# Per-head sums and their spreading in four strips of TensorE: an RWKV and pooling decoder layer

## The chip, the cores and the metric

The kernel runs on one core of a Trainium2 chip. Its time is the device time of one execution in microseconds (us). In this text PE is TensorE (the matrix engine), DVE is VectorE, ACT is ScalarE, POOL is GpSimd and SP is SyncE, which issues the loads here. PE reads its operands from SBUF and writes to PSUM, whose unit here is a bank of 128 rows by 512 numbers of fp32.

## What is computed

One decoder layer on 256 tokens and 2048 channels, all in float32: a mixer, a feed-forward block with squared ReLU, and a gate by a per-layer embedding, each added to the residual stream, with a final norm. Half of the mixer's channels go through causal averages over four windows, the other half, 16 heads of 64 channels, through RWKV-7:

```python
kk = hs(k * k_k)
kk = kk / jnp.maximum(jnp.linalg.norm(kk, axis=-1, keepdims=True), 1e-12)
k = k * (1.0 + (a - 1.0) * k_a)
...
y = wkv7_scan(r_h, hs(decay), k_h, v_h, -kk, kk * a_h)
mu = jnp.mean(y, axis=-1, keepdims=True)
var = jnp.mean(jnp.square(y - mu), axis=-1, keepdims=True)
y = (y - mu) * lax.rsqrt(var + GN_EPS) * gn_g + gn_b
y = y + jnp.sum(r_h * k_h * r_k, axis=-1, keepdims=True) * v_h
```

`hs` splits the channels into heads. The change touches two places of this: the norm of `kk` over the 64 channels of each head (one number for each head and token), which is spread back over the 64 channels, and the last line, a sum over the channels of a head that is spread over them and multiplied by the values. That second term is called the bonus below.

## The kernel before

**Stages.** The mixer fills the first 360 us of the execution, then come the feed-forward block and the gate. Everything after the mixer is the same in both kernels.

**Layout.** The 16 heads are worked on as two groups of 8 (index `gi`, 0 and 1). A group has 512 channels, held as 4 tiles of 128 channels (the partitions) by 256 tokens: `tile[:, p, t]`, p from 0 to 3, two heads in each p. Tiles from the pool `rp` have tags (`tA` to `tF`, `sq` and so on), and a later tile of the same tag waits until the earlier one is no longer read.

**Products of the weights.** A product in full fp32 precision is made of three faster ones: weights and activations are split into a high and a low half (`wh` + `wl`), and `prod_cols` (L176 to L178) and `prod_toks` (L185 to L187) multiply high by high, high by low and low by high. `split_w` makes the halves of a weight panel of 128 x 1024: ACT copies the high half in two pieces (L163), DVE subtracts it to get the low half (L164). The halves lie in rings of three buffers. The products z (`zk`, `zr`, `zv` of each group, and `zp`, the pooled half) take 8 panels each. The small sums and transposes of the mixer are plain fp32 matmuls, for which the trace shows two records each.

**Order.** PE's order is the order of the Python program (`manual_schedule`). The z products are generators in a queue. `fill(us)` takes as many of their products as fill the given time by its own table, 0.36 us for three products of 256 columns and 0.68 for three of 512, and `finish(gen)` runs the queue up to the end of one product. So the order of the main program (L913 to L965) sets at which point of the stream of z products each small step of the mixer stands. The other engines are ordered by a scheduler with priorities: the panels' splits have 20000 and a few steps of `rwkv_k` 30000. `beside` holds a triangular inverse that runs on DVE (L652, L656), one step for each 1.65 us of fill.

**Banks.** The z products use four PSUM banks of the pool `psm`, all small steps of the mixer four of the pool `psr` (`rw_bank`), in turn.

**The norm, `rwkv_k`.** The squares `sq` (ACT) are summed over the heads in 8 fp32 matmuls with the squares as weights and `jhead` (128 x 2, which tells the two heads of a tile) as data (L524); the result has tokens on the partitions and 16 columns. After the maximum and reciprocal on DVE (L527, L529) and the root on ACT, two transposes (L533) bring it to 8 rows (heads) by 256 tokens. These are split into a high half (ACT, L168) and a low half (DVE, `rnp`, L169), and 8 matmuls with `hsel` (L543, L544) spread them over the channels, two tiles p into each of two banks. `kkn` is the product with `zk` and `k_k` (DVE, L548). `rnp` has the tag `tE`, as has `k2`, made from L552 on ACT and L555 on DVE, so `k2` waits for the spreading. `BK` (L567, L568) and `AR` (L569) are built from `kkn` and `k2`.

**The bonus, in `rwkv_values`.** `rk` is the product of r, k and `r_k`. `block_sum` multiplies it by `jsum` (128 x 128, ones where row and column are of one head): sum and spreading in one step, two fp32 matmuls of 512 columns (L463), and DVE multiplies each by the values (L706, `bon`, in the buffer of `rk`). In the same function eight matmuls `vt` (L699) make the centred and transposed values.

**Other steps that are named below.** `rwkv_lora` (L480 to L505): decay and rate of a group, small products `lw` and `la` (L491) into a bank each, then ACT, scans and exponentials. `rwkv_scores` and `rwkv_sources` (`bkt`, L628). `rwkv_merge`: 32 products `gm` (L680) and 32 products `qm` (L687). `rwkv_core`: the recurrence over blocks of 64 tokens (`sm` L767, `rym` L780). `pool_mix`: the pooled half (`pm` on PE, `mp` on ACT L901 and DVE L902).

## Time and profile before

| | us |
|---|---|
| median of three runs | 1205.45 |
| lowest and highest | 1203.94 and 1206.46 |
| the profiled execution, its own time | 1204.86 |
| its span, first to last instruction | 1203.1 |
| PE busy | 1183.2 |
| DVE busy | 872.9 |
| ACT busy | 674.7 |

The mean clock granted to PE is 0.997 of the full one. The trace belongs to the one profiled execution, and what is worked out from it is set against that execution's own time. Rows of the timeline give start, duration, engine, line and operation, then the tiles as out<-in with their sizes and types. A row that ends in square brackets had its engine idle before it, for so long and until the named operation released it. Matmuls overlap in the array, so a row's duration can be longer than the distance to the next row. Rows of the windows give the window, its length, and the busy time of each engine in it with the number of instructions.

### The profile page before, as it was taken

The numbers are of one execution on the slowest core, as the hardware profiler recorded it, in microseconds if no ns is written. First come the engines' busy times: TensorE is split into PE (matmuls) and PEld (weight loads), VectorE is DVE, ScalarE is ACT, GpSimd is POOL, SyncE is SP. The second block draws the span as 40 slices with busy tenths as digits, with TensorE's granted clock in tenths as the row PEclk, the third lists the DMA queues.
The fourth block names the chain that finished last, engine by engine and source line by source line (L and its number), as shares of the span: only waits on it lengthen the run. The fifth ranks groups of instructions, "written<-read, shape, count | busy, mean of one in ns | idle before, by whom it ended". The sixth has DMA issues, their size and how long they took to land.

```text
span 1203.1 us, 18401 instructions
## 1 busy us (share of the span) xinstructions
PE 1183.2 (98%) x7070; PEld 1015.0 (84%) x7070; DVE 872.9 (73%) x1186; ACT 674.7 (56%) x1203; POOL 15.5 (1%) x65
## 2 busy tenths in 40 slices
PE   7999999999999999999999999999999999999997
PEld 5999988987888888888888888888888887887886
DVE  6887987964566666666878887666667788788753
ACT  5957556565545545555545554555555555468743
POOL 3100000000000000000000000000000000000000
PEclk9999999999999999999999999999999999999999
DMA  7363543354365565565656666665565666666841
GB/s 275 124 195 113 175 141 107 107 187 142 120 211 175 175 192 184 185 191 180 192 200 205 206 194 217 185 191 181 187 192 168 194 205 204 229 203 200 271 139 70
DMA packets 60616, 216.88 MB, mean 180 GB/s; under 512 B 6768, under 2 KB 7536, under 8 KB 60144
## 3 DMA queue, kind: packets, MB, share of 16 engines
q1 hardware_dynamic: 60240, 215.20, 55.5%
q8 instruction: 55, 0.90, 0.3%
q10 hardware_dynamic: 288, 0.51, 0.1%
q14 instruction: 33, 0.27, 0.1%
HBM read 213.59 MB, written 2.10 MB: 179 GB/s over the span
## 4 chain that ended last, share of the span: by engine, by line
PE 89%; DVE 6%; DMA 2%; ACT 2%; issue 1%; ACTq 0%; DVEq 0%
PE u_w L1016 20%; PE d_p L1085 15%; PE u_w L1020 10%; PE d_w L1085 4%; PE d_d L1085 4%; DMA raw_d<-in_w_ffn_down_dram 2%; PE gt_b L187 2%; PE gt_b L186 2%; PE gt_b L185 2%; PE wag_b L346 1%; PE zp_b L185 1%; PE zv_b L176 1%; PE zp_b L187 1%; PE zp_b L186 1%; PE o_b L186 1%; PE o_b L185 1%
## 5 line engine op out<-in xcount | busy, mean ns | idle before, releaser
L1016 PE MATMUL u_w<-h,wh_u 128*128 128x512 f32 x1024 | 362.1, 399 | 0.0
L1020 PE MATMUL u_w<-h,wl_u 128*128 128x256 f32 x1024 | 287.7, 281 | 0.0
L164 DVE TENSOR_TENSOR wl_u<-raw_u,wh_u 128x1024 fp32r<-128x1024 f32 x128 | 156.7, 1224 | 122.2 <-ACT wh_u L163 122.2
L163 ACT ACTIVATE wh_u<-raw_u 128x512 fp32r<-128x512 f32 x256 | 147.6, 624 | 173.4 <-issue 137.0
L1016 PEld LDWEIGHTS u_w<-h,wh_u 128*128 128x128 f32 x1024 | 192.4, 188 | 47.9
L1020 PEld LDWEIGHTS u_w<-h,wl_u 128*128 128x128 f32 x1024 | 193.4, 189 | 0.0
L1085 PE MATMUL d_p<-wh_d,yd 128*128 128x512 f32 x480 | 154.5, 389 | 0.8 <-ACT wh_d L163 0.8
L163 ACT ACTIVATE wh_d<-raw_d 128x512 fp32r<-128x512 f32 x160 | 89.1, 620 | 36.8 <-issue 18.5
L1085 PEld LDWEIGHTS d_p<-wh_d,yd 128*128 128x128 f32 x480 | 90.1, 188 | 20.0 <-ACT wh_d L163 1.2
L164 DVE TENSOR_TENSOR wl_d<-raw_d,wh_d 128x1024 fp32r<-128x1024 f32 x80 | 95.4, 1220 | 14.3 <-ACT wh_d L163 13.9
L1085 PE MATMUL d_p<-wl_d,yd 128*128 128x512 f32 x240 | 93.6, 390 | 0.0
L1085 PE MATMUL d_d<-wh_d,yd 128*128 128x512 f32 x160 | 55.8, 389 | 0.0
L1085 PEld LDWEIGHTS d_p<-wl_d,yd 128*128 128x128 f32 x240 | 45.1, 188 | 9.7 <-DVE wl_d L164 0.6
L1138 ACT ACTIVATE th_d<-t_d 128x1024 fp32r<-128x1024 f32 x24 | 25.4, 1058 | 47.6 <-DVE t_d L1135 30.2
L1085 PE MATMUL d_w<-th_d,ys 128*128 128x512 f32 x144 | 48.2, 389 | 0.0
L1142 ACT ACTIVATE th_d<-t_d 128x1024 fp32r<-128x1024 f32 x24 | 25.4, 1059 | 35.4 <-DVE t_d L1140 31.2
L1143 DVE TENSOR_TENSOR tl_d<-t_d,th_d 128x1024 fp32r<-128x1024 f32 x24 | 29.4, 1225 | 19.9 <-ACT th_d L1142 19.6
L1132 ACT ACTIVATE w7h_d<-raw_d 128x1024 fp32r<-128x1024 f32 x24 | 25.4, 1059 | 23.4 <-DMA raw_d<-in_w_ffn_down_dram 13.8
L187 PE MATMUL gt_b<-wh_gt,h 128*128 128x512 f32 x96 | 37.8, 393 | 0.0
L176 PE MATMUL zv_b<-hTh,wh_zv 128*128 128x256 f32 x128 | 37.7, 294 | 0.0
L176 PE MATMUL zr_b<-hTh,wh_zr 128*128 128x256 f32 x128 | 37.5, 293 | 0.0
L185 PE MATMUL gt_b<-wh_gt,h 128*128 128x512 f32 x96 | 37.5, 390 | 0.0
(582 smaller groups left out, 2622.8 us busy)
## 6 DMA issues: line engine op xcount, KB each, us to landing
raw_u<-in_w_ffn_up_dram SPq DMA_DIRECT2D x128, 512.0 KB, 3.5
raw_d<-in_w_ffn_down_dram SPq DMA_DIRECT2D x128, 512.0 KB, 3.9
raw_gt<-in_w_ple_gate_dram SPq DMA_DIRECT2D x24, 512.0 KB, 4.2
raw_zk<-in_w_in_dram SPq DMA_DIRECT2D x16, 512.0 KB, 3.4
raw_zr<-in_w_in_dram SPq DMA_DIRECT2D x16, 512.0 KB, 3.5
raw_zv<-in_w_in_dram SPq DMA_DIRECT2D x16, 512.0 KB, 3.4
raw_zp<-in_w_in_dram SPq DMA_DIRECT2D x16, 512.0 KB, 3.4
raw_o<-in_w_out_dram SPq DMA_DIRECT2D x16, 512.0 KB, 4.1
```

Source lines behind the costliest of these rows:

```text
L163: nc.scalar.activation(wh[:, a * 512 : (a + 1) * 512], raw[:, a * 512 : (a + 1) * 512], AF.Copy)
L164: nc.vector.tensor_tensor(wl, raw, wh.bitcast(F32), op=ALU.subtract)
L176: nc.tensor.matmul(o, w_h, ah, start=first and ct % 2 == 0, stop=False, skip_group_check=True)
L185: nc.tensor.matmul(o, a_h, wh[:, 0:n], start=first, stop=False)
L186: nc.tensor.matmul(o, a_h, wl[:, 0:n], start=False, stop=False)
L187: nc.tensor.matmul(o, a_l, wh[:, 0:n], start=False, stop=last)
L1016: nc.tensor.matmul(bank[:, ct, :].rearrange("p (s t) -> p s t", s=2), wh[:, c], hl, start=k == 0, stop=False, skip_group_check=True,)
L1020: nc.tensor.matmul(bank[:, ct, 0:T], wl[:, c], hl[:, 0, :], start=False, stop=k == 15, skip_group_check=True)
L1085: nc.tensor.matmul(o, l, r, start=first, stop=last, skip_group_check=True)
L1132: nc.scalar.activation(ha, ra, AF.Copy)
L1138: nc.scalar.activation(th[0], t[0], AF.Copy)
L1143: nc.vector.tensor_tensor(tl[1], t[1], th[1].bitcast(F32), op=ALU.subtract)
```

## The change

Sums over a head and their spreading are two steps now, each of four matmuls that use 32 rows or 32 columns of PE's array.

- `head_sums` (new): weights are a slice of 32 columns of `jsel` (128 x 46, zeros with the two head columns in the middle), data a tile of 128 channels by n tokens; the tile p goes to the strip of 32 columns p, that is to the rows 32p to 32p+31 of one bank. For the norm the tokens are cut into 8 pieces of 32, and each piece lands in its own two rows of the strip by the slice of `jsel`: 32 matmuls of 32 columns, and a result of 128 x 32, so that the maximum, the root and the reciprocal work on 32 columns. For the bonus there is one piece: 4 matmuls of 256 columns.
- `head_spread` (new): the rows 32p to 32p+31 of `hsel` (now 128 x 128) as weights and the same rows of the sums as data, four fp32 matmuls of 256 columns, each on its own strip of rows, into four banks.
- In the norm a product with `qmask` on DVE (tile `rnq`, 128 x 256) puts the 8 pieces in their columns. The transposes, the split and the tile `rnp` are gone, and with them the wait of `k2`. The fills become 6.4 and 4.6 (they were 5.4, 3.2 and 1.8).
- The bonus leaves `rwkv_values`. `bonus_sums` stands behind `rwkv_sources`, with a copy to SBUF on ACT; `bonus` spreads the sums and multiplies each bank with the values on DVE, four products of 128 x 256. For group 0 it stands behind a new fill(5.0), ahead of `rwkv_lora(1)`, for group 1 ahead of `rwkv_merge(1)`.
- `rwkv_values(0)` moves from ahead of `rwkv_scores(1)` to behind `rwkv_merge(0)`; the fill behind it is 3.0 (it was 1.5).

```diff
@@ -93,16 +93,15 @@
-    jsum = mc.tile([128, 128], F32, name="jsum")
     cmask = mc.tile([128, 128], F32, name="cmask")
...
     make_block_diagonal(nc, cmask, 64)
-    nc.gpsimd.tensor_copy(jsum, cmask)
     cen = mc.tile([128, 128], F32, name="cen")
-    nc.vector.scalar_tensor_tensor(cen, jsum, -1.0 / 64.0, ident, op0=ALU.mult, op1=ALU.add)
-    jhead = mc.tile([128, 2], F32, name="jhead")
-    nc.gpsimd.tensor_copy(jhead, cmask[:, ::64])
+    nc.vector.scalar_tensor_tensor(cen, cmask, -1.0 / 64.0, ident, op0=ALU.mult, op1=ALU.add)
+    jsel = mc.tile([128, 46], F32, name="jsel")
+    nc.gpsimd.memset(jsel, 0.0)
+    nc.gpsimd.tensor_copy(jsel[:, 14:16], cmask[:, ::64])
@@ -294,12 +293,17 @@
-    hsel_f = rp.tile([8, 512], F32, tag="BKt", name="hsel_f")
-    nc.gpsimd.memset(hsel_f, 1.0)
-    nc.gpsimd.affine_select(hsel_f, hsel_f, [[1, 512]], ALU.is_ge, 0.0, base=0, channel_multiplier=-64)
-    nc.gpsimd.affine_select(hsel_f, hsel_f, [[-1, 512]], ALU.is_ge, 0.0, base=63, channel_multiplier=64)
-    hsel = mc.tile([8, 512], F32R, name="hsel")
-    nc.gpsimd.tensor_copy(hsel, hsel_f)
+    hsel = mc.tile([128, 128], F32, name="hsel")
+    nc.gpsimd.memset(hsel[0:32], 0.0)
+    for q in range(8):
+        nc.gpsimd.affine_select(hsel[0:32], hsel[0:32], [[-1, 2], [0, 64]], ALU.not_equal, 1.0, base=-2 * q, channel_multiplier=1)
+    qmask = mc.tile([128, 8, 32], F32, name="qmask")
+    nc.gpsimd.memset(qmask[0:32], 1.0)
+    nc.gpsimd.affine_select(qmask[0:32], qmask[0:32], [[-2, 8], [0, 32]], ALU.is_ge, 0.0, base=0, channel_multiplier=1)
+    nc.gpsimd.affine_select(qmask[0:32], qmask[0:32], [[2, 8], [0, 32]], ALU.is_ge, 0.0, base=1, channel_multiplier=-1)
+    for p in range(1, 4):
+        nc.gpsimd.tensor_copy(hsel[p * 32 : (p + 1) * 32], hsel[0:32])
+        nc.gpsimd.tensor_copy(qmask[p * 32 : (p + 1) * 32], qmask[0:32])
@@ -455,13 +459,25 @@
-    def block_sum(src, name, consume):
-
-        s = flat(src)
-        for hf in range(2):
-            b = rw_bank("bsum")
-            nc.tensor.matmul(b, jsum, s[:, hf * 512 : (hf + 1) * 512], start=True, stop=True)
-            consume(hf, b)
+    def head_sums(src, name, pieces):
+
+        b = rw_bank(name)
+        n = T // pieces
+        for q in range(pieces):
+            for p in range(4):
+                nc.tensor.matmul(
+                    b[p * 32 : (p + 1) * 32, 0:n], jsel[:, 14 - 2 * q : 46 - 2 * q], src[:, p, q * n : (q + 1) * n],
+                    start=q == 0, stop=q == pieces - 1, skip_group_check=True,
+                )
+        return b[:, 0:n]
+
+    def head_spread(src, name):
+
+        banks = [rw_bank(f"{name}{p}")[:, 0:T] for p in range(4)]
+        for p in range(4):
+            r = slice(p * 32, (p + 1) * 32)
+            nc.tensor.matmul(banks[p], hsel[r], src[r], start=True, stop=True)
+        return banks
 
@@ -512,41 +528,23 @@
                 nc.scalar.activation(sq[:, p, :], zk[:, p, :], AF.Square, scale=col("k_k", 4 * gi + p))
         nc.scalar.activation(warm, sq[:, 3, 0:1], AF.Sqrt)
 
-        fill(5.4)
-        nb = rw_bank("kkn")
...
-        rn = rp.tile([128, 16], F32, tag="rn", name=f"rn{gi}")
+        fill(6.4)
+        nb = head_sums(sq, "kkn", 8)
+        rn = rp.tile([128, 32], F32, tag="rn", name=f"rn{gi}")
+        rnq = rp.tile([128, T], F32, tag="sq", name=f"rnq{gi}")
         with tc.high_priority(30000):
-            nc.vector.tensor_scalar_max(rn, nb[:, 0:16], 1e-24)
+            nc.vector.tensor_scalar_max(rn, nb, 1e-24)
             nc.scalar.activation(rn, rn, AF.Sqrt)
             nc.vector.reciprocal(rn, rn)
-        fill(3.2)
-        nb = rw_bank("rnT")
-        for tt in range(2):
-            nc.tensor.transpose(nb[0:8, tt * 128 : (tt + 1) * 128], rn[:, tt * 8 : tt * 8 + 8], ident)
-        rnh, rnl = (t_[0:8, 0:T] for t_ in pair_tile("tE", f"rnp{gi}"))
-        with tc.high_priority(30000):
-            split_sb(rnh, rnl, nb[0:8, 0:T])
-        fill(1.8)
-        for half in range(2):
-            b = rw_bank("rnb")
...
+            nc.vector.tensor_tensor(
+                rnq.rearrange("r (q t) -> r q t", q=8), rn.unsqueeze(1).to_broadcast([128, 8, 32]), qmask, op=ALU.mult
+            )
+        fill(4.6)
+        rnb = head_spread(rnq, "rnb")
+        for p in range(4):
+            with tc.high_priority(30000):
+                nc.vector.scalar_tensor_tensor(
+                    kkn[:, p, :], zk[:, p, :], col("k_k", 4 * gi + p), rnb[p], op0=ALU.mult, op1=ALU.mult
                 )
@@ -689,6 +687,18 @@
+    def bonus_sums(gi, st):
+        nb = head_sums(st["rk"], "bsum", 1)
+        st["bs"] = rp.tile([128, T], F32, tag="sq", name=f"bs{gi}")
+        with tc.high_priority(30000):
+            nc.scalar.activation(st["bs"], nb, AF.Copy)
+
+    def bonus(st, zv):
+        bon = st["rk"]
+        for p, b in enumerate(head_spread(st["bs"], "bon")):
+            with tc.high_priority(30000):
+                nc.vector.tensor_tensor(bon[:, p, :], b, zv[:, p, :], op=ALU.mult)
+
     def rwkv_values(gi, st, zv):
 
         uvs = [rp.tile([128, 2, 8, 64], F32, tag=f"q{i}", name=f"UV{gi}_{i}") for i in range(2)]
@@ -699,14 +709,6 @@
                 nc.scalar.activation(flat3(UV[2 * tt + i])[64:128], b[i * 64 : (i + 1) * 64, :], AF.Copy)
-        bon = st["rk"]
-        bf, vf = flat(bon), flat(zv)
-        block_sum(
-            st["rk"], f"rk{gi}",
-            lambda hf, b: nc.vector.tensor_tensor(
-                bf[:, hf * 512 : (hf + 1) * 512], b, vf[:, hf * 512 : (hf + 1) * 512], op=ALU.mult
-            ),
-        )
         st["UV"] = UV
 
     def rwkv_core(gi, st):
@@ -929,7 +931,10 @@
     rwkv_scores(0, st0)
     beside += [inverse(0, st0), 1.65, 0.0]
     rwkv_sources(0, st0)
+    bonus_sums(0, st0)
     finish(p_zv0)
+    fill(5.0)
+    bonus(st0, zv0[0])
     st1 = rwkv_lora(1)
     finish(p_zk1)
     rwkv_k(1, st1, zk1[0])
@@ -937,16 +942,17 @@
     rwkv_r(1, st1, zr1[0])
     run(beside.pop(0) if beside else ())
     beside.clear()
-    rwkv_values(0, st0, zv0[0])
     fill(7.0)
     rwkv_scores(1, st1)
     rwkv_merge(0, st0)
     beside += [inverse(1, st1), 0.95, 0.0]
-    fill(1.5)
+    rwkv_values(0, st0, zv0[0])
+    fill(3.0)
     core0 = rwkv_core(0, st0)
     mg0 = a8(0, "mg0", F32R)
     rwkv_out(0, *rwkv_norm1(0, *core0), mg0)
     rwkv_sources(1, st1)
+    bonus_sums(1, st1)
     finish(p_zp0)
     ds0 = pool_chunk(0, pool[0])
     pws0 = pool_weights(0)
@@ -955,6 +961,7 @@
     mixes = [pool_mix(0, ds0, pws0), None]
     run(beside.pop(0) if beside else ())
     beside.clear()
+    bonus(st1, zv1[0])
     rwkv_merge(1, st1)
     rwkv_values(1, st1, zv1[0])
 
```

PE, around the lora of group 1, before: `zv` ends, the lora comes at once, and the products of `zk` for group 1 begin behind it.

```order
L177 MATMUL zv_b_972<-hTl_160,wh_zv_7_1261 128x256
L178 MATMUL zv_b_972<-hTh_158,wl_zv_7_1262 128x256
L491 MATMUL lw<-zf,wa_1322 128x256 x2
L491 MATMUL la<-zf,wa_1322 128x256 x2
L176 MATMUL zk_b_1336<-hTh_157,wh_zk_0_1340 128x256
L177 MATMUL zk_b_1336<-hTl_159,wh_zk_0_1340 128x256
L178 MATMUL zk_b_1336<-hTh_157,wl_zk_0_1341 128x256
```

PE, the same place after: `bsum` stands within the last panel of `zv`, and nearly two panels of `zk` are done when the four spreading matmuls (`bon`) and the lora come.

```order
L176 MATMUL zk_b_1376<-hTl_158,wh_zk_1_1415 128x256
L177 MATMUL zk_b_1376<-hTh_156,wl_zk_1_1416 128x256
L479 MATMUL bon_1440<-bs_1345,hsel 128x256
L479 MATMUL bon_1441<-bs_1345,hsel 128x256
L479 MATMUL bon_1442<-bs_1345,hsel 128x256
L479 MATMUL bon_1443<-bs_1345,hsel 128x256
L507 MATMUL lw<-zf,wa_1452 128x256 x2
L507 MATMUL la<-zf,wa_1452 128x256 x2
L175 MATMUL zk_b_1377<-hTh_156,wh_zk_1_1415 128x256
```

The four `bon` banks are the four of the pool, so that `lw` and `la` take the banks of the first two next.

DVE at that place, before (`tmp` and `X` are steps of the inverse, `wl_zk_3` is the low half of the fourth panel of `zk`, the rows L498 are the lora's scans):

```order
L498 SCALAR_TENSOR_TENSOR tB_t<-rmask,tA_t 128x256
L652 TENSOR_TENSOR tmp_1232<-X_1231,AT_1230 64x175
L498 SCALAR_TENSOR_TENSOR tB_t<-rmask,tA_t 128x256
L656 TENSOR_TENSOR X_1231<-X_1231,tmp_1232 64x7x25
L652 TENSOR_TENSOR tmp_1232<-X_1231,AT_1230 64x192
L498 SCALAR_TENSOR_TENSOR tB_t<-rmask,tA_t 128x256
L656 TENSOR_TENSOR X_1231<-X_1231,tmp_1232 64x8x24
L498 SCALAR_TENSOR_TENSOR tB_t<-rmask,tA_t 128x256
L652 TENSOR_TENSOR tmp_1232<-X_1231,AT_1230 64x207
L656 TENSOR_TENSOR X_1231<-X_1231,tmp_1232 64x9x23
L652 TENSOR_TENSOR tmp_1232<-X_1231,AT_1230 64x220
L164 TENSOR_TENSOR wl_zk_3_1465<-raw_zk_3_1462,wh_zk_3_1464 128x1024
```

DVE there after:

```order
L650 TENSOR_TENSOR tmp_1279<-X_1278,AT_1277 64x175
L654 TENSOR_TENSOR X_1278<-X_1278,tmp_1279 64x7x25
L163 TENSOR_TENSOR wl_zk_3_1531<-raw_zk_3_1528,wh_zk_3_1530 128x1024
L650 TENSOR_TENSOR tmp_1279<-X_1278,AT_1277 64x192
L700 TENSOR_TENSOR ybuf<-bon_1440,zv_t 128x256
L700 TENSOR_TENSOR ybuf<-bon_1441,zv_t 128x256
L654 TENSOR_TENSOR X_1278<-X_1278,tmp_1279 64x8x24
L700 TENSOR_TENSOR ybuf<-bon_1442,zv_t 128x256
L700 TENSOR_TENSOR ybuf<-bon_1443,zv_t 128x256
L650 TENSOR_TENSOR tmp_1279<-X_1278,AT_1277 64x207
```

The bonus products (L700) stand behind `wl_zk_3` and one step of the inverse, and the lora's scans come later.

DVE in the second `rwkv_k`, before, from the transposes that end the inverse (`T1G`) on:

```order
L661 STREAM_TRANSPOSE T1G_1993<-X_1231 32x16x32 x2
L169 TENSOR_TENSOR rnp_1783<-rnT,rnp_1783 8x256
L164 TENSOR_TENSOR wl_zr_5_1876<-raw_zr_5_1873,wh_zr_5_1875 128x1024
L665 STREAM_TRANSPOSE tmp_1232<-X_1231 64x16x32
L548 SCALAR_TENSOR_TENSOR tB_t<-zk_t,par_sb,rnb 128x256 x4
L164 TENSOR_TENSOR wl_zr_6_1909<-raw_zr_6_1906,wh_zr_6_1908 128x1024
L566 TENSOR_TENSOR tF_t<-tB_t,tD_t 128x1024
L555 TENSOR_TENSOR tE_t<-tE_t,zk_t 128x1024
L164 TENSOR_TENSOR wl_zr_7_1944<-raw_zr_7_1941,wh_zr_7_1943 128x1024
L567 TENSOR_TENSOR BK_1828<-tF_t,tC_t 128x16x64
L164 TENSOR_TENSOR wl_zp_0_2027<-raw_zp_0_2024,wh_zp_0_2026 128x1024
L568 TENSOR_TENSOR BK_1828<-tE_t,tC_t 128x16x64
```

DVE there after:

```order
L650 TENSOR_TENSOR tmp_1279<-X_1278,AT_1277 64x135
L553 TENSOR_TENSOR tE_t<-tE_t,zk_t 128x1024
L163 TENSOR_TENSOR wl_zr_2_1791<-raw_zr_2_1788,wh_zr_2_1790 128x1024
L163 TENSOR_TENSOR wl_zr_3_1865<-raw_zr_3_1862,wh_zr_3_1864 128x1024
L566 TENSOR_TENSOR BK_1912<-tE_t,tC_t 128x16x64
L654 TENSOR_TENSOR X_1278<-X_1278,tmp_1279 64x27x5
L536 TENSOR_SCALAR rn_1836<-kkn 128x32
L163 TENSOR_TENSOR wl_zr_4_1925<-raw_zr_4_1922,wh_zr_4_1924 128x1024
L538 RECIPROCAL rn_1836<-rn_1836 128x32
L650 TENSOR_TENSOR tmp_1279<-X_1278,AT_1277 64x112
L539 TENSOR_TENSOR rnq_1837<-rn_1836,qmask 128x256
L654 TENSOR_TENSOR X_1278<-X_1278,tmp_1279 64x28x4
```

The product for `k2` (L553) and the slot of `BK` made from it (L566) stood behind the spreading (L555, L568), and stand now ahead of the norm's steps, with the panels `wl_zr_2` and `wl_zr_4` behind the one and the other.

At the merge of group 1 the four `bon` of group 1 stand between the last product of the pool mix and `gm`, which takes one of their banks next.

More of the change, by code (lines that the diff above doesn't have):

```diff
@@ L513, in rwkv_k @@
         nc.scalar.activation(warm, sq[:, 3, 0:1], AF.Sqrt)
-        fill(5.4)
-        nb = rw_bank("kkn")
-        for hf in range(2):
-            h = flat(sq)[:, hf * 512 : (hf + 1) * 512]
-            for j in range(2):
-                for tt in range(2):
-                    o = tt * 8 + (2 * hf + j) * 2
-                    ts_ = slice(j * T + tt * 128, j * T + (tt + 1) * 128)
-                    first = hf == 0 and j == 0 and tt == 0
-                    nc.tensor.matmul(nb[:, o : o + 2], h[:, ts_], jhead, start=first, stop=True, skip_group_check=True)
@@ L531, in rwkv_k @@
-        nb = rw_bank("rnT")
-        for tt in range(2):
-            nc.tensor.transpose(nb[0:8, tt * 128 : (tt + 1) * 128], rn[:, tt * 8 : tt * 8 + 8], ident)
-        rnh, rnl = (t_[0:8, 0:T] for t_ in pair_tile("tE", f"rnp{gi}"))
-        with tc.high_priority(30000):
-            split_sb(rnh, rnl, nb[0:8, 0:T])
-        fill(1.8)
-        for half in range(2):
-            b = rw_bank("rnb")
-            for j in range(2):
-                p = half * 2 + j
-                o = b[:, j * T : (j + 1) * T]
-                nc.tensor.matmul(o, hsel[:, p * 128 : (p + 1) * 128], rnh, start=j == 0, stop=False, skip_group_check=True)
-                nc.tensor.matmul(o, hsel[:, p * 128 : (p + 1) * 128], rnl, start=False, stop=True, skip_group_check=True)
-            for j in range(2):
-                p = half * 2 + j
-                with tc.high_priority(30000):
-                    nc.vector.scalar_tensor_tensor(
-                        kkn[:, p, :], zk[:, p, :], col("k_k", 4 * gi + p), b[:, j * T : (j + 1) * T], op0=ALU.mult, op1=ALU.mult
+            nc.vector.tensor_tensor(
+                rnq.rearrange("r (q t) -> r q t", q=8), rn.unsqueeze(1).to_broadcast([128, 8, 32]), qmask, op=ALU.mult
+            )
```

## Prediction

> **What bounds the kernel now.** I read the shares by engine first, then the chain of waits, then the waits of TensorE (PE), then the stage of the change (100 to 180 us) in windows.
>
> ```profile
> PE 1183.2 (98%) x7070; PEld 1015.0 (84%) x7070; DVE 872.9 (73%) x1186; ACT 674.7 (56%) x1203; POOL 15.5 (1%) x65
> PE 89%; DVE 6%; DMA 2%; ACT 2%; issue 1%; ACTq 0%; DVEq 0%
> PE rnb L544 <- DVE rnp L169: 0.7, 1, 0.7
> 110.00:120.00 10.00, 10.00 (x83) 9.28 (x80) 9.79 (x24) 9.30 (x18) 0.00 (x0) 1.00 0.30 97
> 120.00:130.00 10.00, 9.93 (x83) 9.72 (x82) 9.59 (x21) 6.06 (x11) 0.00 (x0) 1.00 0.53 166
> 130.00:140.00 10.00, 10.00 (x86) 10.00 (x85) 9.69 (x21) 4.39 (x10) 0.00 (x0) 1.00 0.57 188
> 150.00:160.00 10.00, 10.00 (x71) 9.87 (x71) 9.43 (x12) 5.43 (x10) 1.10 (x2) 0.83 0.44 140
> 152.20:155.40 3.20, 3.20 (x18) 3.20 (x17) 3.20 (x5) 1.66 (x5) 0.00 (x0) 0.50 0.34 129
> 170.00:180.00 10.00, 10.00 (x64) 7.93 (x64) 6.79 (x9) 4.93 (x11) 0.00 (x0) 1.00 0.35 118
> ```
>
> The first two rows say that the end is set by PE's own work: 98% busy, 89% of the chain. So an instruction taken off PE shortens the kernel, unless something else is late behind it. The window rows (length, then busy time of PE, weight load, DVE, ACT, POOL, then the granted clock) say where that may happen: from 110 to 160 us VectorE (DVE) is busy 9.4 to 9.8 of every 10 us. There PE and DVE bound the kernel together, and only after 170 has DVE room again (6.79). Two more things stand in this stage: one wait of PE of 0.7 us in rnb, and a stretch at half clock, 152.2 to 155.4 us, that loses 3.2 x 0.5 = 1.6 us.
>
> How closely PE follows DVE there, two rows tell: the low half of a weight panel is done at 122.31 + 1.21 = 123.52, and PE's first product with it starts at 123.58.
>
> ```profile
> 122.31 1.21 DVE L164 TENSOR_TENSOR wl_zk<-raw_zk,wh_zk 128x1024 fp32r<-128x1024 f32 x1
> 123.58 0.38 PE L178 MATMUL zk_b<-hTh,wl_zk 128*128 128x256 f32 x1
> ```
>
> **What the change takes off PE.** Each block is read from its first row to the first regular product behind it.
>
> ```profile
> 59.02 1.84 PE L524 MATMUL kkn<-jhead,tF_t 128*128 128x2 f32 x16
> 60.72 0.36 PE L176 MATMUL zr_b<-hTh,wh_zr 128*128 128x256 f32 x1
> 64.04 0.38 PE L533 MATMUL rnT<-ident,rn 128*8 128x128 f32 x2
> 66.28 0.28 PE L178 MATMUL zr_b<-hTh,wl_zr 128*128 128x256 f32 x1
> 66.49 0.38 PE L543 MATMUL rnb<-rnp,hsel 8*128 8x256 f32 x1
> 67.62 0.39 PE L176 MATMUL zr_b<-hTh,wh_zr 128*128 128x256 f32 x1
> 148.56 0.38 PE L543 MATMUL rnb<-rnp,hsel 8*128 8x256 f32 x1
> 149.61 0.38 PE L544 MATMUL rnb<-rnp,hsel 8*128 8x256 f32 x1 [0.67 <-DVE rnp L169]
> 150.63 0.39 PE L176 MATMUL zr_b<-hTh,wh_zr 128*128 128x256 f32 x1
> 165.87 1.88 PE L463 MATMUL bsum<-ybuf,jsum 128*128 128x512 f32 x4
> 167.82 0.40 PE L186 MATMUL zp_b<-wl_zp,hTh 128*128 128x512 f32 x1
> ```
>
> There are two groups of heads, so each of these runs twice. Norm sums (kkn): 60.72 - 59.02 = 1.7 us, and 0.1 for the change of shape ahead of it (66.49 - 66.28 = 0.21 us into rnb, where 83 matmuls in a window of 10 us make 0.12 the pace): 1.8, both groups 3.6. Transposes (rnT): between 0.1 and 0.38, I take 0.2, both 0.4; they go altogether. Spreading (rnb): 67.62 - 66.49 = 1.1 and 0.1 ahead, 1.2 in group 0; 150.63 - 148.56 = 2.1 and 0.1 ahead, 2.2 in group 1, which holds the wait. Bonus sums (bsum): 167.82 - 165.87 = 1.95, less about 0.25 for the zp product that lies inside, 1.7; both 3.4. Sum of what goes: 3.6 + 0.4 + 3.4 + 3.4 = 10.8 us.
>
> **What it adds on PE.** The new products work on a 32-wide strip of the array each, and no row of before has four strips. The nearest rows have two, or one:
>
> ```profile
> 45.07 0.48 PE L491 MATMUL lw<-zf,wa 64*128 64x256 f32 x1
> 45.08 0.48 PE L491 MATMUL la<-zf,wa 64*128 64x256 f32 x1
> 45.39 0.38 PE L491 MATMUL lw<-zf,wa 64*128 64x256 f32 x1
> 45.60 0.38 PE L491 MATMUL lw<-zf,wa 64*128 64x256 f32 x1
> 202.58 0.69 PE L767 MATMUL sm<-UV,BKt 128*64 128x64 f32 x16
> 203.11 1.10 PE L780 MATMUL rym<-UV,SC 128*64 128x64 f32 x16
> 204.13 0.39 PE L176 MATMUL zv_b<-hTh,wh_zv 128*128 128x256 f32 x1
> 262.36 2.21 PE L680 MATMUL gm<-T1G,SC 32*32 32x32 f32 x64
> 264.50 0.50 PE L185 MATMUL zp_b<-wh_zp,hTh 128*128 128x512 f32 x1
> ```
>
> lw and la use different halves of the rows of the array and start 0.01 us apart: they run together, and a pair of records takes 45.39 - 45.07 = 0.32 us the first time and 45.60 - 45.39 = 0.21 then. sm alternates between strips, 16 records in 203.11 - 202.58 = 0.53 us; rym has the same shape on one strip, 16 in 1.02. So strips do overlap. An fp32 product leaves two records (64 in the row of gm for 32 products).
>
> A quad of four products of 256 columns (bsum, rnb and bon) is 8 records. If four strips run together it is two such beats, 0.3 and 0.2, and 0.2 for the change of shape in and out: 0.7 us. If they run one after the other it is 0.3 + 7 x 0.2 + 0.2 = 1.9. The pairs say together: I take 0.7. Six quads: 4.2 us. The new kkn is 32 products of 32 columns, 64 records. At the pace of gm, 264.50 - 262.36 = 2.14 us for 64 records on one strip, or 0.033 us each, they take 2.1 and with the shape 2.3; with four strips side by side a quarter, 0.5 and 0.3 for the shape, 0.8. I take 1.0 each, near the lower end because lw and la start 0.01 us apart; both 2.0. The Trainium skill speaks against that: TensorE: Matmul & The Clock Gate, section Back-to-back issue gap, gives a floor of about 25 ns from one product to the next however short it is. By it the 64 records would take an estimated 1.6 us, and the sum below would come out 1.8 us worse; the 10 ns between lw and la are under that floor, the 33 ns of sm are above it.
>
> PE's work: 4.2 + 2.0 - 10.8 = -4.6 us, the 0.7 of the wait among it.
>
> **The half clock.** Of all that PE waits for in this stage only the rnb wait precedes it, by 2.6 us. In the new form there is no transpose between the norms and their spreading: the mask product follows the reciprocal on DVE at once, and 4.6 us of z products cover what 3.2 + 1.8 covered with the transposes between. So I let the wait go, and the half clock with it: -1.6 us. Bounds: 0 and -1.6. The Trainium skill (the same page, section HAM oscillation — how this bites in real kernels) has the clock fall after idle of more than about 3.4 us. By that rule this stretch isn't due to a wait of 0.67 us and would stay, and the sum would be 1.6 us worse; the trace can't decide it: the stretch stands behind that wait, but the wait of h3t, quoted below, has none behind it.
>
> **What it gives back.** The change makes PE wait for DVE at three new places, since the spread takes all four banks of the rw pool at once, and the next user needs DVE to have emptied one.
>
> ```profile
> 112.03 1.21 DVE L164 TENSOR_TENSOR wl_zk<-raw_zk,wh_zk 128x1024 fp32r<-128x1024 f32 x1
> 113.16 0.47 DVE L310 SCALAR_TENSOR_TENSOR zv_t<-zv_b,par_sb,zv_t 128x255 f32<-128x255 f32 x1
> 155.54 1.21 DVE L555 TENSOR_TENSOR tE_t<-tE_t,zk_t 128x1024 f32<-128x1024 f32 x1
> 160.74 1.22 DVE L568 TENSOR_TENSOR BK<-tE_t,tC_t 128x1024 f32<-128x1024 f32 x1
> 170.65 1.27 DVE L706 TENSOR_TENSOR ybuf<-bsum,zv_t 128x512 f32<-128x512 f32 x2
> 262.57 0.89 DVE L902 SCALAR_TENSOR_TENSOR mp<-pm,par_sb,mp 128x256 fp32r<-128x256 f32 x2 [0.54 <-ACT mp L901]
> ```
>
> (a) Bonus of group 0, then lora(1). On DVE the four bonus products stand behind a weight panel (1.21 us) and one small operation of the triangular inverse (0.3); each is a DVE operation of 128x256 out of PSUM, of 0.4 us in a row (0.47 alone, as the zv_t row). lw needs the first bank. If DVE takes the panel when the quad begins, lw waits 1.2 + 0.3 + 0.4 - 0.7 = 1.2 us, and la 0.4 longer behind the second: 1.4 with both. Bounds: 0 if DVE is done with the panel by then, 2.0 if it begins it late. Queued behind on PE is everything; on ACT the lora's exponentials, which have until rwkv_k(1).
>
> (b) DVE work pulled ahead of the second rwkv_k. The bonus moves from 170 us, where DVE has room, to 115, where it has none: 4 x 0.4 = 1.6 us (before, two operations of twice the width, 1.27). The product for k2 (1.21) and the second slot of BK (1.22) no longer wait behind rnp (its tile is gone) and now stand ahead of weight panels of zr, as the order of DVE shows. That is 4.0 us in front of panels, and the one quoted above has a margin of 0.06 us. Against it stand the wait (a), in which DVE catches up, and the rnp pair and two small norms that go. What PE saves before 160 must also be made by DVE: it can't start a panel earlier than DVE has it. Bounds: 0, and 2.4 (the pulled-ahead pair in full). I take 1.0.
>
> (c) Bonus of group 1, then merge(1). gm now needs a bank that DVE empties behind two operations of the pool mix, which end at 262.57 + 0.89 = 263.46; the bonus product makes it 263.9. Without the wait gm would begin the quad's 0.7 later than its 262.36 of before, at 263.1. So about 0.7 us more. Bounds: 0 and 0.9.
>
> What moves without a price: vt of group 0 goes behind merge(0), with fill(3.0) to cover its copies; ACT is 5 to 6 of 10 us busy there. The copies of the bonus sums (a 128x256 on ACT, under 0.5 us each) have 5 us of z products over them; without that cover the first bon would wait 0.5. POOL builds its masks at the start; on SP the lora's weight load moves behind one more panel's load, and its first use behind 5 us more of products.
>
> **The sum.** -4.6 - 1.6 + 1.4 + 1.0 + 0.7 = -3.1 us; from the profiled execution's 1204.86 us (span 1203.1) to 1201.8. That execution is 0.6 below the median of 1205.45, so from the median it would be 1202.4. I take 1202.2.
>
> **Rivals.** (1) The new waits don't come: DVE is ahead where I see it behind, since PE starts a little later at each place. For it: ACT delivers wh early now; against: 9.4 to 9.8 of 10. 1204.86 - 6.2 = 1198.7. (2) DVE swallows it: all that PE saves before 160 is waited for at the panels. What stays are the two bsum quads of 1.7 taken behind 160 (3.4), less the bonus quad and sums of group 1 (1.4) and (c) 0.7, less the bonus's own 1.6 us on DVE now in the bound stretch: -3.4 + 1.4 + 0.7 + 1.6 = +0.3, 1205.2. For it: the 0.06 us margin of the panel; against: at 170 us DVE has room again, and what it does there can slip. (3) Short products issue one after the other: kkn 2.3 each instead of 1.0, 1202.2 + 2.6 = 1204.8. (4) Slower: idle costs clock. One wait of 0.67 us stood ahead of a stretch that lost 1.6. The change has waits at four places (lw of (a), two panels of (b), gm of (c)). With none of them followed by half clock it stands at 1202.2; each that is adds 1.6: 1203.8, 1205.4, 1207.0, 1208.6. From the second on nothing is won, at the third it is slower. For it: the stretch at 152; against: the longest wait on another engine, at h3t, where no half clock follows:
>
> ```profile
> 1101.31 0.66 PE L1037 MATMUL h3t<-ident,x 128*128 128x128 f32 x4 [0.82 <-DVE h L1044]
> 1104.00:1108.00 4.00, 4.00 (x23) 3.26 (x22) 2.91 (x7) 3.87 (x11) 0.00 (x0) 1.00 0.43 141
> ```
>
> (5) Four strips don't run together: 6 x 1.2 + 2.6 = 9.8 more, 1212.0; against: sm at half the time of rym. (6) The change doesn't do what it says for the wait: rnq is as late as rnp was, and the wait and the half clock stay: 1202.2 + 0.7 + 1.6 = 1204.5.
>
> **How the numbers follow.** About 0.2% (2.4 us) is what a measurement tells from no change. Forecast 0.42, with its own range from 1200.8 to 1203.6; rival 1 0.22; 2 0.11; 3 0.06; 4 0.12; 5 0.03; 6 0.04. Faster (under 1203.0): 0.36 of the forecast and all of 1, 0.58. Same: 0.06 of the forecast, 0.09 of rival 2, all of 3 and 6, 0.25. Slower: 4, 5 and the rest of 2, 0.17. The range goes from 1198.6 to 1207.2: it takes in 1 to its point and 4 up to its third step, and leaves out 5, the end of 4 and the lower side of 1.
>
> **What would show it.** Right: the spread quads as 8 records within 0.8 us, four starts within 0.05 us; kkn near 1.0; no PE wait at rnb and a clock of 1.00 in all windows from 140 to 170; PE waits of about a microsecond at lw (on DVE's bonus) and 0.7 at gm. Wrong: a quad of 1.9 us; kkn over 2; new rows of half clock behind the lw wait; PE waits on wl_zk or wl_zr that add up to more than 2 us; or no waits at all at lw and gm.

## The result and the profile after

The changed kernel takes 1207.22 us (median of 17 runs, 1205.35 to 1212.11); before took 1203.94 (17 runs, 1200.04 to 1206.48). The ratio is 1.0036, with a 95% interval from 1.0024 to 1.0047: slower, by 3.3 us by the medians and about 4 by the ratio. The profiled execution took 1207.79 us, with a span of 1206.1.

TensorE's own work first. In the timeline of after, the new blocks:

```profile
60.34 0.28 PE L177 MATMUL zr_b<-hTh,wl_zr 128*128 128x256 f32 x1
60.55 0.76 PE L468 MATMUL kkn<-tF_t,jsel 128*32 128x32 f32 x64
61.24 0.39 PE L175 MATMUL zr_b<-hTh,wh_zr 128*128 128x256 f32 x1
66.10 0.71 PE L479 MATMUL rnb<-rnq,hsel 32*128 32x256 f32 x8
66.75 0.39 PE L175 MATMUL zr_b<-hTh,wh_zr 128*128 128x256 f32 x1
114.09 0.71 PE L479 MATMUL bon<-bs,hsel 32*128 32x256 f32 x8
115.86 0.70 PE L507 MATMUL lw<-zf,wa 64*128 64x256 f32 x2 [1.06 <-DVE ybuf L700]
```

The norm's sums, 64 records, take 61.24 - 60.55 = 0.69 us, where the 16 records of before took 1.7; a spreading quad 66.75 - 66.10 = 0.65. With 0.1 each for the change of shape in and out the two are 0.9 and 0.8. The four strips do run side by side. So the work shrank as forecast. The waits of PE from 50 to 270 us tell where it went (us in total, times, longest):

```profile
PE zr_b L177 <- DVE wl_zr L163: 1.4, 3, 0.6
PE zp_b L185 <- DVE wl_zp L163: 1.4, 1, 1.4
PE zk_b L177 <- DVE wl_zk L163: 1.2, 1, 1.2
PE lw L507 <- DVE ybuf L700: 1.1, 1, 1.1
PE gm L678 <- DVE tF_t L700: 0.5, 1, 0.5
PE rym L740 <- DVE sbd L780: 0.4, 1, 0.4
```

6.0 us in eight waits, where before had the 0.7 of rnb. The view counts idle time only; from start to start, less the pace of 0.12 (0.23 for zp), the same eight cost 7.4 us, as 171.31 - 169.55 - 0.23 = 1.5 for zp. The windows show the holes in PE, and that DVE was hardly busier than before in sum:

```profile
110.00:120.00 10.00, 8.94 (x71) 7.52 (x70) 9.73 (x25) 6.20 (x13) 0.00 (x0) 1.00 0.39 118
120.00:130.00 10.00, 8.80 (x74) 8.60 (x72) 9.69 (x21) 9.64 (x18) 0.00 (x0) 1.00 0.17 52
170.00:180.00 10.00, 8.70 (x59) 6.80 (x60) 9.46 (x13) 6.32 (x15) 0.00 (x0) 1.00 0.58 172
50.00:180.00 130.00, 124.98 (x1132) 116.64 (x1131) 111.18 (x185) 82.82 (x159) 1.10 (x2) 1.00 0.49 154
268.20:271.50 3.30, 3.30 (x10) 2.65 (x9) 0.44 (x1) 1.74 (x3) 0.00 (x0) 0.51 0.00 0
```

The same window of before, for the fourth row:

```profile
50.00:180.00 130.00, 129.12 (x1034) 122.42 (x1034) 110.02 (x181) 83.33 (x159) 1.10 (x2) 0.99 0.47 152
```

DVE works 111.2 us there and worked 110.0. The last row of after is the half clock: the stretch at 152 is gone, and a new one of the same length stands at 268, some 2 us behind the wait of gm. The end of the mixer, the last product of o_b before its wait for the residual, before and after:

```profile
392.97 0.39 PE L187 MATMUL o_b<-wh_o,mp 128*128 128x512 f32 x1
```

```profile
395.11 0.39 PE L186 MATMUL o_b<-wh_o,mp 128*128 128x512 f32 x1
```

So 2.1 us of the loss are there in this pair of executions, each of which has one stretch at half clock. The rest is not traced: from that row to the end, where the kernels are the same, the fourteen profiled executions of this study took from 806.1 to 811.8 us, so a difference of a few us between two totals says little. Over the 17 runs the mean granted clock of after is 0.9965; over the runs of before that belong to the experiments it is 0.9975. A thousandth of 1204 us would be an estimated 1.2 us of PE; whether it is lost here is taken up behind the steps of the prediction.

**The wait at the third zp panel** has the longest chain. DVE, then ACT, then PE in after:

```profile
142.17 1.21 DVE L553 TENSOR_TENSOR tE_t<-tE_t,zk_t 128x1024 f32<-128x1024 f32 x1
145.57 1.21 DVE L566 TENSOR_TENSOR BK<-tE_t,tC_t 128x1024 f32<-128x1024 f32 x1
152.62 1.12 DVE L659 STREAM_TRANSPOSE T1G<-X 32x512 f32<-32x512 f32 x1
164.02 1.18 DVE L663 STREAM_TRANSPOSE tmp<-X 64x512 f32<-64x512 f32 x1
167.90 0.87 DVE L314 SCALAR_TENSOR_TENSOR zr_t<-zr_b,par_sb,zr_t 128x255 f32<-128x255 f32 x2 [1.62 <-ACT zr_t L313]
170.03 1.22 DVE L163 TENSOR_TENSOR wl_zp<-raw_zp,wh_zp 128x1024 fp32r<-128x1024 f32 x1
```

```profile
165.23 2.13 ACT L667 ACTIVATE SC<-tmp 32x1024 f32<-32x1024 f32 x2 [2.12 <-DVE tmp L663]
167.39 0.84 ACT L313 ACTIVATE zr_t<-zr_b,omu 128x256 f32<-128x256 f32 x2
```

```profile
169.55 0.39 PE L184 MATMUL zp_b<-wh_zp,hTh 128*128 128x512 f32 x1
171.31 0.50 PE L185 MATMUL zp_b<-wl_zp,hTh 128*128 128x512 f32 x1 [1.36 <-DVE wl_zp L163]
```

DVE before:

```profile
147.31 2.00 DVE L661 STREAM_TRANSPOSE T1G<-X 32x512 f32<-32x512 f32 x2
164.13 0.48 DVE L310 SCALAR_TENSOR_TENSOR zr_t<-zr_b,par_sb,zr_t 128x255 f32<-128x255 f32 x1
166.40 1.21 DVE L164 TENSOR_TENSOR wl_zp<-raw_zp,wh_zp 128x1024 fp32r<-128x1024 f32 x1
```

k2 and its slot of BK go ahead of the last steps of the triangular inverse. The inverse's first closing transpose is at 152.62, which was at 147.31 before. Its copies on ACT (2.13 us) then stand in front of zr_t, zr_t comes on DVE at 167.90 in place of 164.13, DVE idles 1.62 us for it, and wl_zp stands behind zr_t (170.03, before 166.40). Meanwhile PE is there sooner: before, vt and bsum lay ahead of zp, now neither does.

### The profile page after: what moved, and what is told of

Same layout as the page of the kernel before. It is cut to its first block, busy times and chain, and to the rows that moved or that the text cites. A ratio compares the mean times of both kernels' runs of the same rounds, so it can differ in the third digit from the quotient of the medians.

```text
span 1206.1 us, 18657 instructions
## 1 busy us (share of the span) xinstructions
PE 1181.2 (98%) x7186; PEld 1010.6 (84%) x7186; DVE 873.7 (72%) x1190; ACT 675.8 (56%) x1203; POOL 21.3 (2%) x79
## 4 chain that ended last, share of the span: by engine, by line
PE 76%; DVE 12%; DMA 6%; ACT 3%; issue 2%; DVEq 0%; ACTq 0%
PE u_w L1023 20%; PE u_w L1027 10%; PE d_p L1092 9%; DMA raw_d<-in_w_ffn_down_dram 5%; PE d_d L1092 2%; PE d_w L1092 2%; PE gt_b L186 2%; PE gt_b L184 2%; PE gt_b L185 2%; PE wag_b L350 2%; PE o_b L185 1%; PE o_b L184 1%; PE o_b L186 1%; DVE wl_d L163 1%; PE zp_b L184 1%
## 5 line engine op out<-in xcount | busy, mean ns | idle before, releaser
L177 PE MATMUL zr_b<-hTh,wl_zr 128*128 128x256 f32 x128 | 36.5, 285 | 1.4 <-DVE wl_zr L163 1.4
```

Of the source, the lines that this page charges most:

```text
L177: nc.tensor.matmul(o, w_l, ah, start=False, stop=last, skip_group_check=True)
```

## The experiments

Three theories were set against each other. **A**: order. Work of DVE and ACT was moved ahead of something that PE needs, and work of PE that covered a late panel was moved away; each wait has its own cause. **B**: sum. Between 110 and 170 us DVE sets the pace, and what PE saves it must wait for, wherever things stand. **C**: clock. The waits bring stretches at half clock behind them, in some executions more than in others.

| kernel | median us | ratio to before | 95% interval | PE waits, 50 to 270 us | mean clock of the runs |
|---|---|---|---|---|---|
| before | 1203.94 | | | 0.7 | 0.9975 |
| changed | 1207.22 | 1.0036 | 1.0024 to 1.0047 | 6.0 | 0.9965 |
| e1 norm only | 1202.04 | 0.9983 | 0.9971 to 0.9995 | 1.4 | 0.9982 |
| e2 bonus only | 1204.18 | 1.0005 | 0.9991 to 1.0018 | 2.7 | 0.9970 |
| e3 late bonus | 1206.88 | 1.0029 | 1.0015 to 1.0042 | 4.5 | 0.9961 |
| e4 k2 held | 1204.66 | 1.0003 | 0.9989 to 1.0018 | 4.6 | 0.9973 |
| e5 values back | 1203.70 | 1.0005 | 0.9990 to 1.0020 | 3.8 | 0.9968 |
| e6 strips only | 1207.66 | 1.0030 | 1.0014 to 1.0046 | 4.1 | 0.9962 |
| e7 norm, k2 held | 1202.12 | 0.9991 | 0.9979 to 1.0004 | 2.1 | 0.9981 |
| e8 moved only | 1203.66 | 1.0004 | 0.9994 to 1.0015 | 1.7 | 0.9980 |
| e9 norm, fill | 1200.38 | 0.9979 | 0.9966 to 0.9992 | 0.8 | 0.9984 |
| e10 bonus 1 early | 1204.13 | 1.0009 | 0.9997 to 1.0021 | 5.2 | 0.9982 |
| e11 k2 held, values back | 1202.38 | 1.0000 | 0.9986 to 1.0014 | 4.2 | 0.9968 |
| e12 placed | 1198.92 | 0.9965 | 0.9951 to 0.9980 | 1.3 | 0.9981 |

The waits are idle times of one profiled execution, the other columns stand for 7 to 17 runs. Each ratio is to the runs of before that belong to it (medians 1204.00 for e1 to e4, 1204.09 for e5 to e8, 1202.94 for e9 to e12).

**e1, the norm alone.**

```diff
-    bonus_sums(0, st0)
     finish(p_zv0)
-    fill(5.0)
-    bonus(st0, zv0[0])
...
+    rwkv_values(0, st0, zv0[0])
     fill(7.0)
...
```

`rwkv_values` has the bonus by `jsum` in it again, for both groups, and the fill of 1.5 is back.

> The norm in four strips as in the changed kernel; the bonus as one product with the 128 x 128 matrix, in its place of before, and the values of group 0 in their place of before. Theory A (the strips save on TensorE what was worked out, and the loss comes from places where DVE or ACT work was moved ahead of something TensorE needs): no wait at lw and none over 0.3 us at wl_zk; the wait of 0.8 us at the third zr panel of group 0 stays, and about 0.5 us at a zr panel behind the early k2; the norm's matmuls are 3.5 to 4 us shorter; time 2 to 3 us under before. Theory B (between 110 and 170 us DVE sets the pace in sum, so that whatever TensorE saves is waited for): within 1 us of before, with new waits at the weight panels of 3 us and more in sum. Theory C (the loss is the clock): waits as in A, and a stretch at half clock of 3.4 us decides.

Measured: 2 us under before; waits of 0.6 us (zr, group 0), 0.5 (zk) and 0.3 (kkn). A's number, though the wait at zk is over A's 0.3 and the one behind the early k2 did not come. Half of the change is a gain.

**e2, the bonus and the moves alone** (norm with transposes).

> The norm as before, with transposes; the bonus in strips, ahead of the lora of group 1 and of the merge of group 1, and the values of group 0 behind the merge, as in the changed kernel. Theory A: the waits at lw (1.3 us), at the sixth zk panel (1.4 us), at the third zp panel (1.5 us) and at gm (0.7 us) are there as in the changed kernel, against 0.4 us that the quads save: 3 to 5 us slower than before. Theory B: 1 to 2 us slower, since the extra DVE work in the stage is only 0.4 us and the order does not matter. Theory C: no more than 2 us slower.

Measured: as before, within the interval. The waits at lw (1.1), zk (0.7) and gm (0.5) are there, the one at zp is not: A missed by about 3 us, and what B and C expected lies within the interval. Norm and bonus cost 6 us more together than the sum of e1 and e2, so something needs both.

**e3, the bonus of group 0 late.**

```diff
-    fill(5.0)
-    bonus(st0, zv0[0])
     st1 = rwkv_lora(1)
...
+    bonus(st0, zv0[0])
     rwkv_values(0, st0, zv0[0])
```

> The changed kernel, with the spreading of the bonus of group 0 behind the merge of group 0 (ahead of its values) and without the new fill of 5.0, so that the lora of group 1 comes at once behind zv as before; the sums stay where they are, in a tile of their own. Theory A: the waits at lw and at the sixth zk panel go, 2.7 us; those at the zr panels, zp and gm stay; 2 to 3.5 us under the changed kernel. Theory B: within 1 us of the changed kernel, the same waits at other panels.

Measured: as slow as the changed kernel. The waits at lw and at the sixth zk panel are gone, but PE comes sooner to the panels behind them, and those have not gained as much. The third zr panel of group 1 is there 1.2 us earlier (143.40, in after 144.57), and PE still waits 1.4 us for it in place of 0.4. A new wait of 0.5 stands at vt, behind the four banks of the bonus:

```profile
PE zr_b L177 <- DVE wl_zr L163: 2.0, 2, 1.4
PE zp_b L185 <- DVE wl_zp L163: 1.5, 1, 1.5
```

A missed, and B's number came: removing the first wait only moves it down the stream as long as the late panels stay late.

**e4, k2 held behind the spreading again.**

```diff
-        sq, kkn, k2 = e4("tF"), e4("tB"), e4("tE")
+        sq, kkn = e4("tF"), e4("tB")
...
-        rnq = rp.tile([128, T], F32, tag="sq", name=f"rnq{gi}")
+        rnq = e4("tE")[:, 0, :]
...
+        k2 = e4("tE")
```

> The changed kernel, with the masked norms in the buffer of k2, so that k2 waits for the spreading again and its product and its slot of BK come behind it on DVE, as before. Theory A: the waits of 0.5 us each at two zr panels go, and those at lw, zk, zp and gm stay: 0.5 to 1.2 us under the changed kernel. Theory B: no change within 0.5 us.

Measured: 1.0003 in place of 1.0036, 2.6 us by the medians and 4 by the ratios, more than the 1.2 us. Neither theory had it: the waits at zr are even longer (2.0), but the one at zp is gone. The waits of the stage fall by 1.4 us in sum; the rest of the gain is not traced. On DVE in e4 the inverse is done early and wl_zp stands at 167.39, not at 170.03:

```profile
146.85 1.11 DVE L660 STREAM_TRANSPOSE T1G<-X 32x512 f32<-32x512 f32 x1
167.39 1.21 DVE L163 TENSOR_TENSOR wl_zp<-raw_zp,wh_zp 128x1024 fp32r<-128x1024 f32 x1
```

**e5, the values of group 0 back ahead of zp.**

```diff
+    rwkv_values(0, st0, zv0[0])
     fill(7.0)
     rwkv_scores(1, st1)
     rwkv_merge(0, st0)
     beside += [inverse(1, st1), 0.95, 0.0]
-    rwkv_values(0, st0, zv0[0])
-    fill(3.0)
+    fill(1.5)
```

> The changed kernel, with the values of group 0 (eight matmuls, 1.9 us on TensorE) and the fill of 1.5 back in their places of before, ahead of the scores of group 1. Theory A (order: what was moved uncovers single waits): the wait of 1.5 us at the third zp panel goes, since the values again lie ahead of it, and nothing else changes: 1 to 1.7 us under the changed kernel. Theory B (DVE's pace in sum): within 0.7 us of it, the wait is split among later panels.

Measured: 1.0005. The low half is as late as in after (170.15), but the 1.9 us of vt stand ahead and there is no wait at zp:

```profile
170.15 1.23 DVE L163 TENSOR_TENSOR wl_zp<-raw_zp,wh_zp 128x1024 fp32r<-128x1024 f32 x1
164.24 1.95 PE L709 MATMUL vt<-cen,zv_t 128*128 128x128 f32 x16
```

The gain by the ratio, 3 to 4 us, is again more than this wait. So the zp wait needs both: the panel made late by k2 and its cover taken away. It is absent in e1, e2, e4 and e5 and, below, in e8, e11 and e12, which lack one of the two or both, and present in e3 and e10, which have both. With the two zr waits of group 1, absent in e1 and e2 as well, it makes 2.6 us from start to start of the 6 that norm and bonus cost only together; the rest is not traced.

**e6, all strips, nothing moved** (bonus behind the values; its sums stay behind `rwkv_sources`, as in the changed kernel).

> The four-strip form of all six sums and spreadings, and nothing moved: the bonus of either group behind its values in their places of before, no new fill, k2 behind the spreading, fills 5.4 and 5.0 in the norm (before 5.4, 3.2 and 1.8). Theory A: TensorE keeps its 4.7 us less of work, with waits under 1.5 us in sum in the stage from 50 to 180 us: 2.5 to 4 us under before. Theory B: waits at weight panels of 3 us and more in sum, within 1 us of before.

Measured: 0.3% slower. The place was bad for a reason of its own: the quad wants four banks at once, and two of them hold vt until ACT has copied it. The clock is halved from 166.0, within the wait, to 172.8:

```profile
166.55 1.74 PE L479 MATMUL bon<-bs,hsel 32*128 32x256 f32 x4 [2.33 <-ACT UV L712]
168.00:172.00 4.00, 4.00 (x10) 3.01 (x10) 2.97 (x6) 0.00 (x0) 0.00 (x0) 0.50 0.24 90
```

Both theories missed: it speaks neither for A nor for B, and shows what the quad needs.

**e7, e1 with k2 held and fills 5.4 and 5.0.**

> The norm in strips alone (bonus in its old form and place), with k2 behind the spreading and fills 5.4 and 5.0. Theory A: the wait of 0.8 us at the third zr panel of group 0 and those behind the early k2 go, so it is 0.5 to 1.2 us under the kernel with the norm alone (1202.0), 2.5 to 3.5 us under before. Theory B: the same as the kernel with the norm alone, within 0.5 us.

Measured: no gain over e1. The wait in group 0 is gone, and waits of 2.1 us at zr have come in its place: with the norm alone an early k2 does no harm. A's number missed, and B's came.

**e8, the moves without strips** (the bonus as two matmuls of 512 columns, in its new places).

> The kernel of before with nothing in strips, but with the moves: the bonus in its old form (two matmuls of 512 columns) behind a fill of 5.0 and ahead of the lora of group 1, and ahead of the merge of group 1; the values of group 0 behind its merge, with a fill of 3.0. Theory A: waits at lw or la, at a zk panel (over 0.7 us) and at gm as in the changed kernel: 1.5 to 3.5 us slower than before. Theory B: within 1 us of before, since the DVE work is the same.

Measured: as before, within 0.2%, so A missed and B's number came. It has the wait at zk (1.3) but none at lw or gm: two banks leave the next step a free one. The waits at lw and gm belong to the four banks of the strip form.

**e9, e1 with fills 5.4 and 5.6 in group 0.**

> The norm in strips alone, with k2 early, and in group 0 the fills 5.4 and 5.6 in place of 6.4 and 4.6. Theory A (single waits, each with its own cause): the wait of 0.8 us at the third zr panel of group 0 goes, since the norm's sums stand again ahead of that panel; the other waits stay at about 1 us in sum; 0.3 to 1 us under the kernel with the norm alone, 2.3 to 3.3 us under before. Theory B (DVE's pace in sum): the 0.8 us come back at later panels, 2 us under before as with 6.4 and 4.6.

Measured: 0.9979; 0.6 us of waits gone and none come back. The gain over e1 is within the noise, the sign and the waits are A's.

**e10, the bonus of group 1 ahead of the pool mix.**

```diff
     finish(p_zv1)
+    bonus(st1, zv1[0])
     fill(4.0)
...
-    bonus(st1, zv1[0])
     rwkv_merge(1, st1)
```

> The changed kernel, with the spreading of the bonus of group 1 ahead of the fill of 4.0 and the pool mix, no longer directly ahead of the merge. Theory A: the wait of 0.75 us at gm goes, nothing else moves before 255 us: 0.7 us under the changed kernel. Theory C (a wait of TensorE brings the half clock behind it in a part of the executions): the stretch at half clock behind gm goes with it, and the mean clock of the runs, 0.9965 in the changed kernel, rises by about 0.001: 1.5 to 2.5 us under the changed kernel.

Measured: 1.0009 in place of 1.0036; by the medians, each against its own runs of before, 1.2 us slower in place of 3.3. So 2 to 3 us for a wait of 0.75. The window behind gm is at full clock, and the mean clock of the runs went from 0.9965 to 0.9982. C's number; whether the clock is the reason is taken up behind the steps of the prediction.

```profile
266.00:270.00 4.00, 4.00 (x67) 3.33 (x64) 1.21 (x3) 2.90 (x6) 0.00 (x0) 1.00 0.10 37
```

**e11, e4 and e5 together.**

> The changed kernel, with k2 behind the spreading and the values of group 0 in their place of before, both together. Alone the one took 2.5 us off, the other 3.5. Theory A (both act through one wait, that of 1.5 us at the third zp panel, which either removes): together no more than 1 us beyond the better of the two, within 1 us of before. Theory B (each gives DVE room of its own): the gains add up, 5 us and more under the changed kernel, 1.5 to 2.5 us under before.

Measured: 1.0000, against 1.0003 and 1.0005: the gains don't add. A: both act through one wait.

**e12, strips everywhere, each at a place where nobody waits.**

```diff
-        fill(6.4)
+        fill(6.4 if gi else 5.4)
...
-        fill(4.6)
+        fill(4.6 if gi else 5.6)
...
-    fill(5.0)
-    bonus(st0, zv0[0])
     st1 = rwkv_lora(1)
+    fill(3.0)
+    bonus(st0, zv0[0])
...
+    rwkv_values(0, st0, zv0[0])
     fill(7.0)
...
-    rwkv_values(0, st0, zv0[0])
-    fill(3.0)
+    fill(1.5)
...
     finish(p_zv1)
+    bonus(st1, zv1[0])
     fill(4.0)
```

> All six sums and spreadings in strips, placed where nobody waits for them: the bonus of group 0 behind the lora of group 1 and a fill of 3.0, the values of group 0 in their place of before, the bonus of group 1 ahead of the fill of 4.0, fills 5.4 and 5.6 in group 0; k2 early. Theory A: no wait at lw and gm, none over 0.5 us at the zk panels, the wait at the third zr panel of group 0 gone; waits of 1 to 2 us in sum remain: 2 to 3.5 us under before. Theory B: waits at weight panels of 3 us and more in sum, within 1 us of before.

Measured: 0.9965 (0.9951 to 0.9980), 4 us under before and 8 under the changed kernel.

```profile
PE zr_b L177 <- DVE wl_zr L163: 1.0, 2, 0.6
PE kkn L468 <- ACT tF_t L528: 0.3, 1, 0.3
50.00:180.00 130.00, 128.61 (x1163) 120.09 (x1163) 111.71 (x185) 84.30 (x162) 1.10 (x2) 1.00 0.49 156
```

DVE does 111.7 us of work in this window, no less than in the changed kernel (111.2), and PE is busy 128.6 of 130. B falls: with the same sum the waits shrink from 6.0 to 1.3 us, so the limit here was the order. It is the fastest kernel of the study, level with e9 within the intervals.

## Why the prediction was wrong

The forecast was 1202.2, 3.2 us (0.3%) under the median of three that before had then; the result is 0.36% slower, at 1207.22 just beyond the upper end of the range (1207.2), which rested on rival 4. The miss is larger than these times tell, since before itself came out 1.5 us lower over its 17 runs: 3.2 us faster was forecast, and 3.3 slower was measured. By its steps:

- **PE's work, -4.6: right.** The norm's sums measure 0.9 (forecast 1.0), the quads 0.8 (0.7). By the floor of about 25 ns that the Trainium skill gives (TensorE: Matmul & The Clock Gate, section Back-to-back issue gap) a kkn block would be an estimated 1.8 with the change of shape. Its 64 records in 0.69 us are 11 ns apart on four strips, so here the measurement decides against it.
- **(a) lw, 1.4, and (c) gm, 0.7: right**, 1.3 and 0.75 from start to start.
- **(b), "I take 1.0", bounds 0 and 2.4: the step that failed.** The waits at weight panels cost 4.8 us in after: 0.8 at zr in group 0, 1.4 at the sixth zk panel, 0.5 and 0.5 at zr in group 1, 1.5 at zp. The bound counted the DVE work that was put in front of panels. It didn't count that work behind is displaced too (the inverse by k2, and zr_t behind the inverse's copies; the lora's exponentials behind lw, and a panel's high half behind them on ACT), nor the PE work that had covered a late panel. For zp the runs show both; what holds up the zk and zr panels is read from the order in the trace, and only for zk a run bears on it (e3).
- **"What moves without a price: vt of group 0": wrong.** It was the cover of the third zp panel; e5, which puts it back, is 3 to 4 us faster by the ratio, 1.5 of them this wait. The fills of 6.4 and 4.6, which the prediction didn't price, moved the norm's sums behind the third zr panel of group 0, which ACT delivers no sooner: 0.8 us, gone in e6, e7, e9 and e12, which have 5.4 there.
- **The half clock, -1.6: wrong.** The rnb wait and the stretch behind it went, but a stretch of the same length came at 268 in this execution, so that nothing was won. Rival 4 named this mechanism, and rival 2 the waits at the panels; the second is in the trace as 4.8 us, how much the first cost beyond before is not shown.
- The wait at rym (0.6 from start to start) was not foreseen.

In sum -4.6 of work and +7.4 of waits make +2.8 from the mixer. The two o_b rows show 2.1, and 0.2 for an earlier start (the first lw product is at 44.89, before at 45.07); the 0.5 between is not traced.

The clock column of the table parts the kernels by one thing. Those in which gm waits for DVE (the changed kernel, e2, e3, e4, e5, e11) run at 0.9961 to 0.9973; those without it (e1, e7, e8, e9, e10, e12) at 0.9980 to 0.9984, though e10 has the other waits, 5.2 us of them. e6, with its wait within the bon quad, is at 0.9962, and before, with the wait within rnb, at 0.9975. In the profiled executions the stretch stands behind gm in the changed kernel, e2 and e11 (3.4 us) and e5 (10.2), and is missing behind the same wait of 0.5 us in e3 and e4; the kernels without that wait have none behind gm. So the half clock follows the wait at gm in a part of the executions.

It would be near to say that a wait does it when it stands next to matmuls on narrow strips. The wait at lw speaks against that. It is twice as long (1.0 to 1.1 us), stands between the bon quad (32 rows) and lw (64 rows), and the clock behind it is 1.00 in all six traces that have it. First e10 behind lw, then e3 behind gm:

```profile
114.00:122.00 8.00, 6.96 (x55) 5.54 (x54) 7.76 (x19) 4.72 (x11) 0.00 (x0) 1.00 0.41 134
266.00:270.00 4.00, 4.00 (x68) 3.35 (x64) 1.37 (x4) 2.80 (x5) 0.00 (x0) 1.00 0.02 4
```

Nor is the mean clock a price. In every trace the clock is also halved at the end, 2 to 5 us behind PE's last matmul, where that costs PE nothing: for 3.1 us in before and 6.0 in after, which by itself makes the difference between their 0.997 and 0.996. And the three executions of the changed kernel at 0.998 or 0.999 took 1206.96, 1206.99 and 1207.17 us, within 0.3 of its median. So the loss does not need the clock.

Not settled: what sets gm, rnb and the bon quad of e6 apart from lw (no run changed the shape of the matmuls next to a wait), and how much of e10's gain is the clock. By the o_b rows its mixer ends 2.0 us before that of the changed kernel, and the stretch of 3.4 us there is 1.7 of them; but all its twelve executions are at 0.998 or above, with a median of 1204.13, and the changed kernel's three at such a clock took 1207.

## What to carry to other kernels

When a saving on one engine is planned beside an engine that delivers just in time, the question is not only what is added ahead of the deliveries: ask what the removed or moved work had covered, and which queue the moved work now stands in, two or three links down. A form that takes all buffers of a pool at once makes its neighbours wait for whoever empties them; put it where the next user is far off. And a saving should be tried with its placement free: the same six blocks were worth +4 us in one order and -4 in another.
